# Recurrent gates on 64 x 64 quarters of TensorE, a weight tile for two blocks, and ScalarE's first copies and casts in program order

## The chip, the cores and the metric

The kernel runs on one core of one Trainium2 chip. Its engines are TensorE (PE, with its weight load PEld), VectorE (DVE), ScalarE (ACT), GpSimd (POOL) and SyncE (SP, which issues the DMAs here). The metric is the device time of one execution, in microseconds (us).

## The reference

Two layers of a hybrid model over 256 tokens and 256 context tokens, width 1024. Each layer normalises and modulates its input, projects it with one wide matrix, feeds three mixers (a bidirectional gated linear recurrence, retention, windowed attention), merges them and adds a mixture of 32 experts. The change lies in the norm's start and in the recurrence (LRU), whose gates are products with 16 matrices of 64 x 64, one for each head:

```python
def lru_scan(u, wa, ba, wx, bx, lam, h0, reverse):
    ub = u.reshape(B, L, LRU_HEADS, LRU_BW)                # 16 heads of 64
    r = jax.nn.sigmoid(jnp.einsum('blhi,hij->blhj', ub, wa).reshape(B, L, D_RNN) + ba)
    i = jax.nn.sigmoid(jnp.einsum('blhi,hij->blhj', ub, wx).reshape(B, L, D_RNN) + bx)
    log_a = -LRU_C * r * jax.nn.softplus(-lam)
    a = jnp.exp(log_a)
    b = jnp.sqrt(-jnp.expm1(2.0 * log_a)) * (i * u)
    a_cum, b_cum = lax.associative_scan(_linear_combine, (a, b), reverse=reverse, axis=1)
    return a_cum * h0[:, None, :] + b_cum
```

## The kernel before

Everything is kept transposed: channels on the 128 partitions, 512 tokens (context, then latent) along the free axis. Weights come in as fp32 tiles `raw` of 1 MB, and each half of one is split by ScalarE (`whi`, a cast) and VectorE (`wlo`, the rest), so that TensorE multiplies three times, `whi` with `uhi` and `ulo`, and `wlo` with `uhi`. `Dense.T` (L207 to L209) does that for 256 output channels in four groups of 12 matmuls, `Dense.N` (L258 to L260) for products with tokens on the partitions, and `Dense.first` (L238 to L240) for the first 512 channels of a layer, in two halves of the contraction, so that the second half of the norm's output may come later. In layer 0 `norm1` makes its scale and shift in two halves: `mod_half` multiplies four 1 MB tiles `wmod` by the condition (psmod, L441, four column tiles of the array), adds a bias on VectorE (modrow, L445), transposes on TensorE (pst, L447) and copies (modT, L450); ScalarE and VectorE then each modulate half the tokens (u, L561 and L562), and a cast and a subtraction make `uhi` and `ulo` (L488, L489). The second half runs as `between()` inside `first`.

`lru` runs four blocks of 256 channels. A block projects, convolves (`lu`, L606 on ScalarE and L610 on VectorE) and appends to a list `pend` four `gates(kk, di)`, one `root` and two `scan(kk)`; `tick()`, called after each group of 12 matmuls, takes one of them from the list. A gate is two fp32 matmuls of 128 x 128 by 512 (zr L622, zi L623; each shows as two records), two Tanh on the PSUM banks (tr L625, ti L631), a Tanh and an Exp (lT L627, lQ L628), and two VectorE steps. `root` is one Sqrt over a whole block (L648, behind a table load). `scan` is VectorE's row of products and scans (L655 to L667). Two heads share a 128 x 128 weight, whose other two quarters are zeros: `load_lru_w` has GpSimd clear the tile `lruw` (L578), and eight DMAs of 32 KB fill its diagonal, once for each block. Between these, single `psmod` groups (L412, from `mod_vec`) fill in as work that later stages need; each multiplies a 1 MB `wmod` tile, of which there are two buffers.

A scheduler sets one fixed order of instructions for each engine ahead of time, from the program, buffer sizes and its own costs; `tc.keep_in_program_order` holds chosen instructions in the order in which the program names them. Each DMA waits in SyncE's order. So what stands ahead of an instruction on its engine can hold it up.

## Time and profile before

| | |
|---|---|
| median of 3 runs | 2469.4 us (2464.6 to 2470.68) |
| the profiled execution | 2469.8 us, of which the span is 2468.0 |
| TensorE busy | 2332.3 us, 95% of the span |
| VectorE busy | 1273.3 us, 52% |
| ScalarE busy | 784.8 us, 32% |
| GpSimd busy | 69.9 us, 3% |

Busy times are averages over stages with different limits. The layer-0 recurrence lies at about 59 to 200 us of the span, that of layer 1 at about 1440 to 1612 us; the experts follow each. The rest of the kernel is not touched by the change.

### The profile page before, as it was taken

Reading aid. Unit: us, or ns where it says so; the run is one execution under the profiler, and the core shown is the slowest. Engines: PE = TensorE matmul, PEld = TensorE weight load, DVE = VectorE, ACT = ScalarE, POOL = GpSimd, SP = SyncE. Lnnn points to the kernel's source line nnn. Section 1 sums busy time; section 2 is a strip of 40 time slices with the busy share of each in tenths; the row PEclk is TensorE's granted clock in tenths of the full one; section 3 lists DMA queues with packets and bytes.
Section 4 is the critical chain, followed back from the end, with each engine's and each line's share of the span. In section 5 each row is a group of like instructions: output and inputs, shape, how many; then the busy total and the mean of one; then the engine's idle time right before and its main releaser. Section 6 shows DMA issues by size and latency. Waiting matters only on the chain. (4 is left out here: it accounts for less than half of the span.)

```text
span 2468.0 us, 33524 instructions
## 1 busy us (share of the span) xinstructions
PE 2332.3 (95%) x13576; PEld 1586.1 (64%) x13576; DVE 1273.3 (52%) x2458; ACT 784.8 (32%) x1397; POOL 69.9 (3%) x99
## 2 busy tenths in 40 slices
PE   6999999999999989998999989999999889989997
PEld 5667787888888964445444367788889844333433
DVE  4796444367764552324233678776787632222224
ACT  3665222255543321000000166744555411010001
POOL 1000000000000000000000110000000000000001
PEclk8999999999999979999999989999999989999999
DMA  8655353221323557999899932233334889999997
GB/s 291 234 188 198 132 187 102 86 86 52 96 86 106 186 219 303 398 389 376 364 399 415 376 99 90 86 103 120 120 104 147 311 344 405 419 383 420 420 420 293
DMA packets 203709, 589.44 MB, mean 239 GB/s; under 512 B 24112, under 2 KB 135328, under 8 KB 154656
## 3 DMA queue, kind: packets, MB, share of 16 engines
q1 hardware_dynamic: 203552, 587.26, 62.6%
q8 instruction: 109, 1.79, 0.3%
q14 instruction: 48, 0.39, 0.1%
HBM read 585.05 MB, written 2.16 MB: 238 GB/s over the span
## 5 line engine op out<-in xcount | busy, mean ns | idle before, releaser
L180 DVE TENSOR_TENSOR wlo<-raw,whi 128x1024 fp32r<-128x1024 f32 x212 | 258.9, 1222 | 215.6 <-ACT whi L179 209.6
L179 ACT CAST whi<-raw 128x1024 fp32r<-128x1024 f32 x212 | 222.5, 1050 | 353.6 <-PE pT L208 283.3
L207 PE MATMUL pT<-uhi,whi 128*128 128x512 f32 (+1 forms) x896 | 331.0, 370 | 2.3 <-ACT uhi L488 2.3
L209 PE MATMUL pT<-uhi,wlo 128*128 128x512 f32 (+1 forms) x896 | 315.6, 352 | 0.0
L208 PE MATMUL pT<-ulo,whi 128*128 128x512 f32 (+1 forms) x896 | 315.0, 352 | 0.0
L1239 PE MATMUL pdn<-we,hT 128*64 128x512 f32 x1024 | 260.6, 607 | 35.9 <-DMA we<-in_expert_w_down_dram 35.9
L1239 PE MATMUL pup<-we,xT 128*64 128x512 f32 x1024 | 231.5, 593 | 1.5 <-DMA we<-in_expert_w_up_dram 1.5
L1239 PE MATMUL pgate<-we,xT 128*64 128x512 f32 x1024 | 231.0, 603 | 0.0
L1239 PEld LDWEIGHTS pdn<-we,hT 128*64 128x64 f32 x1024 | 83.7, 139 | 203.4 <-issue 129.5
L207 PEld LDWEIGHTS pT<-uhi,whi 128*128 128x128 f32 x896 | 169.7, 190 | 39.0 <-issue 12.6
L208 PEld LDWEIGHTS pT<-ulo,whi 128*128 128x128 f32 x896 | 169.8, 190 | 26.1 <-issue 4.9
L209 PEld LDWEIGHTS pT<-uhi,wlo 128*128 128x128 f32 x896 | 169.3, 189 | 25.1 <-issue 1.1
L1328 ACT CAST myh<-pdn 128x512 fp32r<-128x512 f32 x64 | 37.6, 587 | 457.2 <-PE pdn L1239 457.2
L1239 PEld LDWEIGHTS pup<-we,xT 128*64 128x64 f32 x1024 | 75.2, 137 | 150.7 <-issue 143.7
L1239 PEld LDWEIGHTS pgate<-we,xT 128*64 128x64 f32 x1024 | 71.3, 139 | 140.1 <-issue 137.2
L258 PE MATMUL pN<-whi,uhi 128*128 128x256 f32 x512 | 151.2, 295 | 0.0
L259 PE MATMUL pN<-wlo,uhi 128*128 128x256 f32 x512 | 145.6, 284 | 5.6 <-DVE wlo L180 5.5
L1329 DVE TENSOR_TENSOR myl<-pdn,myh 128x512 fp32r<-128x512 f32 x64 | 44.0, 688 | 198.1 <-ACT myh L1328 198.1
L260 PE MATMUL pN<-whi,ulo 128*128 128x256 f32 x512 | 145.4, 284 | 0.0
L207 PE MATMUL pT<-yhi,whi 128*128 128x512 f32 (+1 forms) x384 | 132.4, 345 | 0.0
L209 PE MATMUL pT<-yhi,wlo 128*128 128x512 f32 (+1 forms) x384 | 129.4, 337 | 0.0
L208 PE MATMUL pT<-ylo,whi 128*128 128x512 f32 (+1 forms) x384 | 129.4, 337 | 0.0
(335 smaller groups left out, 3995.6 us busy)
## 6 DMA issues: line engine op xcount, KB each, us to landing
we<-in_expert_w_down_dram SPq DMA_DIRECT2D x128, 1024.0 KB
we<-in_expert_w_gate_dram SPq DMA_DIRECT2D x127, 1024.0 KB
we<-in_expert_w_up_dram SPq DMA_DIRECT2D x125, 1024.0 KB
raw<-in_w_in_dram SPq DMA_DIRECT2D x76, 1024.0 KB
wmod<-in_w_mod_dram SPq DMA_DIRECT2D x48, 1024.0 KB
raw<-in_w_branch_a_dram SPq DMA_DIRECT2D x8, 1024.0 KB
raw<-in_w_branch_b_dram SPq DMA_DIRECT2D x8, 1024.0 KB
raw<-in_w_branch_c_dram SPq DMA_DIRECT2D x8, 1024.0 KB
```

The costliest lines, as they stand in the source:

```text
L179: act.copy(hi, raw[:, 4 * kh:4 * kh + 4])
L180: dve.tensor_sub(lo, raw[:, 4 * kh:4 * kh + 4], hi.bitcast(F32))
L207: pe.matmul(ps[j], wh, xhi(kk)[:, n0:n1], start=kk == 0, stop=False)
L208: pe.matmul(ps[j], wh, xlo(kk)[:, n0:n1], start=False, stop=False)
L209: pe.matmul(ps[j], wl, xhi(kk)[:, n0:n1], start=False, stop=kk == 7)
L258: pe.matmul(ps[:, i], xh, wh, start=kk == 0, stop=False)
L259: pe.matmul(ps[:, i], xh, wl, start=False, stop=False)
L260: pe.matmul(ps[:, i], xl, wh, start=False, stop=kk == 7)
L1239: keep(pe.matmul(*a, **k))
L1328: act.copy(yh[:, cc], pd)
L1329: dve.tensor_sub(yl[:, cc], pd, yh[:, cc].bitcast(F32))
```

## The change

Four edits go together. (1) `lruw` holds the matrices of two blocks without zeros, [128, 4, 4, 64]; eight DMAs of 64 KB fill it, for blocks 0 and 1 ahead of the norm and for blocks 2 and 3 in block 1; the clearing on GpSimd is gone. (2) A gate is four matmuls of 64 x 64 by 512 on the four quarters of the array: zr on (0, 0) and (64, 64), zi on (0, 64) and (64, 0), so that zi's two halves come out with their partitions exchanged. (3) ti's Tanh is two instructions on 64 partitions each, reading the exchanged halves. (4) `Dense.half` makes the parts of `first`; its casts are held in program order, as are the first copies of `norm1` (L546), and the first half of the first weight tile is cast ahead of the first modulation.

```diff
+        def half(self, c, kh):
+            raw = self.raws[c][:, 4 * kh:4 * kh + 4]
+            hi = T("ws", [P, 4, 256], F32R, name="whi")
+            lo = T("ws", [P, 4, 256], F32R, name="wlo")
+            tc.keep_in_program_order(act.copy(hi, raw))
+            dve.tensor_sub(lo, raw, hi.bitcast(F32))
+            return hi, lo
...
-                    act.copy(hi, self.raws[c][:, 4 * kh:4 * kh + 4])
-                    dve.tensor_sub(lo, self.raws[c][:, 4 * kh:4 * kh + 4], hi.bitcast(F32))
-                    parts.append((hi, lo))
+                    parts.append(self.early.pop() if kh + c == 0 else self.half(c, kh))
...
-                (act.copy if k % 2 else dve.tensor_copy)(us[k], pss[k])
+                tc.keep_in_program_order((act.copy if k % 2 else dve.tensor_copy)(us[k], pss[k]))
         if early:
             vectors(0)
+            dns[0].early = [dns[0].half(0, 0)]
...
-        wb = lru_w[L, c] = T("t4", [P, 2, 4, P], name="lruw")
-        ms = pool.memset(wb, 0.0)
-        if L and c == 0:
-            tc.keep_in_program_order(ms)
+        wb = T("t4", [P, 4, 4, 64], name="lruw")
+        for i in range(2):
+            lru_w[L, c + i] = wb[:, 2 * i:2 * i + 2]
...
-        if c < 3:
-            load_lru_w(L, c + 1)
+        if c == 1:
+            load_lru_w(L, 2)
...
-            pe.matmul(zr, wb[:, kk, 2 * di], uf, start=True, stop=True)
-            pe.matmul(zi, wb[:, kk, 2 * di + 1], uf, start=True, stop=True)
+            for h, z in ((0, zr), (1, zr), (0, zi), (1, zi)):
+                r, o = 64 * h, 64 * (h if z is zr else 1 - h)
+                pe.matmul(z[o:o + 64], wb[r:r + 64, kk, 2 * di + (z is zi)], uf[r:r + 64], start=True, stop=True,
+                          tile_position=(r, o))
...
-            act.activation(ti, zi, AF.Tanh, scale=0.5, bias=vt[:, 64 + 8 * di + k:65 + 8 * di + k])
+            for r in (0, 64):
+                act.activation(ti[r:r + 64], zi[64 - r:128 - r], AF.Tanh, scale=0.5,
+                               bias=vt[r:r + 64, 64 + 8 * di + k:65 + 8 * di + k])
```

The order of instructions moves at three places. In the listings a row gives the line, the operation, and its output and inputs by name with a running number.

The first is VectorE at the first modulation of layer 0, before:

```order
L362 COPY lam_92<-vec_245 128x16
L445 TENSOR_TENSOR modrow_316<-psmod_251,bmod_96 128x128
L450 COPY modT_55_320<-pst_318 128x4x2
L557 SCALAR_TENSOR_TENSOR a_50_249<-modT_55_320,vec_245 128x2x4
L445 TENSOR_TENSOR modrow_322<-psmod_250,bmod_110 128x128
L450 COPY modT_58_326<-pst_324 128x4x2
L562 TENSOR_SCALAR u_231<-u_231,a_50_249,modT_58_326 128x256 x2
```

and after:

```order
L367 COPY lam_92<-vec_244 128x16
L219 TENSOR_TENSOR wlo_249<-raw_124,whi_248 128x1024
L450 TENSOR_TENSOR modrow_319<-psmod_254,bmod_96 128x128
L450 TENSOR_TENSOR modrow_325<-psmod_253,bmod_110 128x128
L455 COPY modT_57_323<-pst_321 128x4x2
L563 SCALAR_TENSOR_TENSOR a_52_252<-modT_57_323,vec_244 128x2x4
L455 COPY modT_60_329<-pst_327 128x4x2
```

The first `wlo`, which needs the first `raw` tile and its cast, now stands ahead of both modrow; before, it came well behind the four modulations.

The second place is the second half of `first` in layer 0. TensorE before:

```order
L441 MATMUL psmod_466<-wmod_134,sT 32x128 x16
L447 MATMUL pst_534<-cst,modrow_532 128x128
L447 MATMUL pst_539<-cst,modrow_537 128x128
L238 MATMUL pT_406<-uhi_189,whi_559 128x512
L238 MATMUL pT_407<-uhi_189,whi_559 128x512
L238 MATMUL pT_408<-uhi_189,whi_563 128x512
```

TensorE after:

```order
L452 MATMUL pst_523<-cst,modrow_521 128x128
L452 MATMUL pst_528<-cst,modrow_526 128x128
L417 MATMUL psmod_572<-wmod_573,sT 32x256 x8
L243 MATMUL pT_399<-uhi_188,whi_548 128x512
L244 MATMUL pT_399<-ulo_189,whi_548 128x512
L243 MATMUL pT_400<-uhi_188,whi_548 128x512
L244 MATMUL pT_400<-ulo_189,whi_548 128x512
L417 MATMUL psmod_572<-wmod_595,sT 32x256
```

SyncE's issues that feed it, before:

```order
L170 DMA raw_567<-in_w_in_dram 128x8x256
L170 DMA raw_569<-in_w_in_dram 128x8x256
L310 DMA wmod_584<-in_w_mod_dram 128x2x1024
L310 DMA wmod_606<-in_w_mod_dram 128x2x1024
L323 DMA bmod_638<-in_b_mod_dram 4x256 x2
L310 DMA wmod_628<-in_w_mod_dram 128x2x1024
```

and after:

```order
L128 DMA am_390<-in_const_dram 128x256
L1050 DMA br_7739<-in_router_group_b_dram 128x4
L1050 DMA br_7739<-in_router_expert_b_dram 128x32
L315 DMA wmod_573<-in_w_mod_dram 128x2x1024
L315 DMA wmod_595<-in_w_mod_dram 128x2x1024
L315 DMA wmod_617<-in_w_mod_dram 128x2x1024
L170 DMA raw_556<-in_w_in_dram 128x8x256
L170 DMA raw_558<-in_w_in_dram 128x8x256
```

Two psmod groups with new wmod tiles now stand ahead of or among the first matmuls of that half; SyncE issues those tiles ahead of the two `raw`, behind `am` and two small loads (`br`). Before, both groups came behind the half. On ScalarE the last two casts of `first` (whi_548 and whi_552 after, whi_559 and whi_563 before), which stood ahead of the second modulation, now stand behind it.

The third place is ScalarE at the end of the last LRU block of layer 0, its last two gates and what follows, before:

```order
L625 ACTIVATE tr_1618<-zr_1614,vec_245 128x512
L631 ACTIVATE ti_1623<-zi_1615,vec_245 128x512
L627 ACTIVATE lT_1551<-tr_1618,spm 128x512
L628 ACTIVATE lQ_1552<-tr_1618,spm 128x512
L625 ACTIVATE tr_1644<-zr_1640,vec_245 128x512
L631 ACTIVATE ti_1649<-zi_1641,vec_245 128x512
L627 ACTIVATE lT_1551<-tr_1644,spm 128x512
L628 ACTIVATE lQ_1552<-tr_1644,spm 128x512
L494 ACTIVATE rk_1652<-pT_1537 128x512
```

and after:

```order
L631 ACTIVATE tr_1640<-zr_1634,vec_244 128x512
L638 ACTIVATE ti_1645<-zi_1635,vec_244 64x512
L633 ACTIVATE lT_1565<-tr_1640,spm 128x512
L634 ACTIVATE lQ_1566<-tr_1640,spm 128x512
L638 ACTIVATE ti_1645<-zi_1635,vec_244 64x512
L631 ACTIVATE tr_1669<-zr_1663,vec_244 128x512
L638 ACTIVATE ti_1674<-zi_1664,vec_244 64x512
L633 ACTIVATE lT_1565<-tr_1669,spm 128x512
L634 ACTIVATE lQ_1566<-tr_1669,spm 128x512
L638 ACTIVATE ti_1674<-zi_1664,vec_244 64x512
L499 ACTIVATE rk_1678<-pT_1551 128x512
```

Each gate has one ti more, and `rk`, the first ScalarE step of the retention, now follows all eight halves of the block. In blocks 1 and 2 the gates have the same form, and a cast `whi` with its `wlo`, which stood among the gates, now stands between `lu` and the table load.

## Rows read from the trace of the kernel before

**Rows 1.** Windows, layer 0: stretch, us, then each engine's busy us

```profile
98.00:133.00 35.00, 35.00 (x182) 23.27 (x181) 31.14 (x47) 23.43 (x31) 0.31 (x1) 1.00 0.56 190
```

**Rows 2.** Timeline (start us, duration us, instruction), ScalarE, one layer-0 LRU block

```profile
115.59 0.81 ACT L627 ACTIVATE lT<-tr,spm 128x512 f32<-128x512 f32 x1
...
117.01 0.67 ACT L631 ACTIVATE ti<-zi,vec 128x512 f32<-128x512 f32 x1
117.58 0.67 ACT L625 ACTIVATE tr<-zr,vec 128x512 f32<-128x512 f32 x1
...
150.81 0.81 ACT L627 ACTIVATE lT<-tr,spm 128x512 f32<-128x512 f32 x1
```

**Rows 3.** Timeline, VectorE, the same block's scan

```profile
130.99 0.68 DVE L655 SCALAR_TENSOR_TENSOR lT<-lQ,lT 128x512 f32<-128x512 f32 x1
```

**Rows 4.** Timeline, TensorE, first gates of blocks 1 and 2 of layer 0

```profile
106.40 1.02 PE L622 MATMUL zr<-lu,lruw 128*128 128x512 f32 x2
...
140.37 1.02 PE L622 MATMUL zr<-lu,lruw 128*128 128x512 f32 x2
```

**Rows 5.** Timeline, TensorE, the first work behind the layer-0 LRU

```profile
196.34 1.18 PE L498 MATMUL prot<-rk,dcr 128*128 128x256 f32 x4 [2.11 <-ACT rk L494]
```

**Rows 6.** Groups by line and form, ScalarE: 64 partitions, then 128

```profile
L929 ACT CAST aq<-aq 64x512 fp32r<-64x512 f32 x16 | 9.9, 620 | 15.1 <-DVE aq L502 14.9
...
L952 ACT CAST yhi<-ya 128x512 fp32r<-128x512 f32 x8 | 4.5, 617 | 0.0
```

**Rows 7.** Timeline, TensorE, the first gate of layer 0 and what surrounds it

```profile
66.10 1.07 PE L412 MATMUL psmod<-wmod,sT 128*32 128x256 f32 x16
67.10 0.50 PE L207 MATMUL pT<-uhi,whi 128*128 128x512 f32 x1
67.44 0.39 PE L208 MATMUL pT<-ulo,whi 128*128 128x512 f32 x1
67.67 0.40 PE L209 MATMUL pT<-uhi,wlo 128*128 128x512 f32 x1
...
71.19 1.02 PE L622 MATMUL zr<-lu,lruw 128*128 128x512 f32 x2
72.05 1.02 PE L623 MATMUL zi<-lu,lruw 128*128 128x512 f32 x2
73.00 1.07 PE L412 MATMUL psmod<-wmod,sT 128*32 128x256 f32 x16
```

**Rows 8.** Timeline, TensorE, first gates of two successive blocks of layer 1

```profile
1497.03 1.10 PE L622 MATMUL zr<-lu,lruw 128*128 128x512 f32 x2 [0.86 <-issue]
...
1535.49 1.10 PE L622 MATMUL zr<-lu,lruw 128*128 128x512 f32 x2 [0.74 <-ACT rv L778]
```

**Rows 9.** Timeline, ScalarE, one of the waits inside that block

```profile
1504.56 0.69 ACT L625 ACTIVATE tr<-zr,vec 128x512 f32<-128x512 f32 x1 [0.28 <-PE zr L622]
```

**Rows 10.** Timeline, TensorE, between the start and the second half of `first`

```profile
23.76 1.94 PE L441 MATMUL psmod<-wmod,sT 128*32 128x128 f32 x32 [3.06 <-DMA wmod<-in_w_mod_dram]
...
32.10 0.79 PE L238 MATMUL pT<-uhi,whi 128*128 128x512 f32 x1 [5.11 <-ACT whi L225]
...
34.19 0.79 PE L240 MATMUL pT<-uhi,wlo 128*128 128x512 f32 x1 [0.87 <-DVE wlo L226]
...
54.74 1.20 PE L238 MATMUL pT<-uhi,whi 128*128 128x512 f32 x4 [1.90 <-ACT uhi L488]
```

**Rows 11.** Timeline, ScalarE, the same stretch

```profile
26.95 1.09 ACT L561 ACTIVATE u<-u,modT,a 128x256 f32<-128x256 f32 x2 [8.14 <-DVE modT L450]
...
35.79 1.99 ACT L225 CAST whi<-raw 128x1024 fp32r<-128x1024 f32 x2 [1.17 <-DMA raw<-in_w_in_dram]
```

**Rows 12.** Timeline, SyncE's issues, the weights behind the first half

```profile
51.80 1.73 SPq L170 DMA_DIRECT2D raw<-in_w_in_dram  x2
```

**Rows 13.** DMA in 40 slices of 0.5 us, from 50 to 70 us

```profile
GB/s 81 15 6 64 36 60 150 207 315 381 389 369 334 272 276 350 362 354 377 389 401 410 401 410 410 410 434 401 358 191 74 0 0 0 0 0 106 106 303 377
```

**Rows 14.** Windows: busy time of each engine, granted clock (PEclk), at layer 1's start

```profile
1434.00:1440.00 6.00, 5.99 (x15) 4.77 (x16) 5.99 (x12) 4.85 (x10) 0.00 (x0) 0.51 0.23 50
```

More of the change, by code (lines that the diff above doesn't have):

```diff
@@ L222, in first @@
                 for c in range(2):
-                    hi = T("ws", [P, 4, 256], F32R, name="whi")
-                    lo = T("ws", [P, 4, 256], F32R, name="wlo")
-                    act.copy(hi, self.raws[c][:, 4 * kh:4 * kh + 4])
-                    dve.tensor_sub(lo, self.raws[c][:, 4 * kh:4 * kh + 4], hi.bitcast(F32))
-                    parts.append((hi, lo))
+                    parts.append(self.early.pop() if kh + c == 0 else self.half(c, kh))
                 if kh:
@@ L583, in load_lru_w @@
                 for par in range(2):
-                    nc.sync.dma_start(
-                        wb[64 * par:64 * par + 64, :, 2 * di + ty, 64 * par:64 * par + 64],
-                        A[nm][L, di, 4 * c + par:4 * c + 4:2].rearrange("k i j -> i k j"))
+                    nc.sync.dma_start(wb[64 * par:64 * par + 64, :, 2 * di + ty],
+                                      A[nm][L, di, 4 * c + par:4 * c + 8:2].rearrange("k i j -> i k j"))
     def lru(L, dn, u, q0, between):
```

## The prediction

> **What bounds the kernel now.** I read the windows first, then the timelines of the stretches that the change touches, engine by engine, then the groups by form for prices. In the layer-0 recurrence TensorE shows no gap: 35.00 us busy of 35.00, with ScalarE at 23.43 [rows 1]. That looks like a stretch in which shorter matmuls are worth their whole length. The timelines say otherwise. From lT of one block to lT of the next, ScalarE and VectorE form a closed chain: ScalarE runs four gates without a gap from 115.59 on, then lu, a table load and the Sqrt [rows 2]; VectorE's scan takes over at 130.99 [rows 3] and runs without a gap to gx, ScalarE's gx and a cast follow, and the next lT starts at 150.81 [rows 2]. That is 35.22 us a block, more than TensorE's own period, 33.97 from the first gate of block 1 to that of block 2 [rows 4]. At the end TensorE indeed waits 2.11 us for ScalarE's rk [rows 5]. In layer 1 the chain closes through TensorE: first gates of two blocks are 38.46 us apart [rows 8], and TensorE waits inside. So in blocks 1 to 3 of both layers ScalarE's time counts, and TensorE's does so only in the first block, where ScalarE waits for each zr, and where gates hold ScalarE up.
>
> **Part 1, the gates on TensorE.** zr and zi start 0.86 us apart, so a gate takes 1.72, of two passes of 0.43 for each matrix [rows 7]. No row of before shows quarters. The nearest are column tiles: psmod, 16 records of 256 columns on four column tiles, takes 1.00 us from its start to the next matmul [rows 7]; at 0.215 a pass, four at a time make 0.86, so four column tiles run at once, with 0.14 for changing the array's form; 0.09 more ahead of the group (zi to psmod takes 0.95 instead of 0.86) and 0.11 behind it (67.10 to 67.44 is 0.34, the next step to 67.67 only 0.23) make 0.35. If four quarters run at once, a gate is 0.86 + 0.35 = 1.21, a gain of 0.51, or 16.3 us over 32 gates. If two do, 2.07, a loss of 0.35; if none do, 3.44 + 0.35, a loss of 2.07. The trace has no two row tiles next to each other, so it can't show how they do together. I take 1.21, since psmod is nearest in kind, and keep the others as a rival. Little of the gain lies on the path: three gates of block 0 in each layer, 3 x 0.51 = 1.5 us, and in layer 1 the waits of ScalarE for zr and zi within a block, of which one shows 0.28 [rows 9] and the three together 0.6.
>
> **Part 2, ti in halves.** On ScalarE a cast of 64 x 512 takes 620 ns, one of 128 x 512 takes 617 [rows 6]: partitions are free, and a half costs what the whole did. The step from ti to the next instruction is 0.57 us [rows 2]. Bounds: nothing, if halves went twice as fast, which those rows exclude, and 0.67, the duration. Four gates a block add 4 x 0.57 = 2.3 us, back to back, ahead of the Sqrt. In block 0 only the last half counts, 0.57. The cover that could hide this, ScalarE's idle time during the scan, lies behind the chain's next step, since lT stands behind gx in the order.
>
> **Part 3, casts moved in blocks 1 and 2.** whi now stands between lu and the table load; that leaves ScalarE's sum as it was, but its wlo comes on VectorE ahead of the scan's first step, and by my chain ends some 0.3 later than the Sqrt. Another wlo goes into the scan's stretch (about 1.15) while its whi leaves the place ahead of lT (about 0.95): +0.2. Together +0.5 for each of the two.
>
> **Part 4, the start of layer 0.** Before, modrow ended the wait and u began at 26.95 [rows 11]. Now the first wlo stands ahead of both modrow on VectorE, and its wait for raw holds them, pst on TensorE, u on ScalarE and all behind. When does raw land? Its predecessor landed at 23.76 [rows 10], the raw three tiles later at 35.79 [rows 11]: 12.03 us for 4 MB, about 3.0 each, so 26.8. The cast and wlo need about 2.6 more, so modrow comes at 29.4 and u at about 30.9, nearly 4 us later. Against this the cast is done, and TensorE's first half, which began at 32.10 [rows 10] and then stopped for wlo to 34.19 [rows 10], begins at about 32.5 and has no such stop: it ends some 1.5 us earlier, near 47, and the second u comes near 51.6. But the casts whi that stood ahead of that modulation are now behind it, so TensorE has both operands near 56.8, against 54.74 [rows 10]. Worse, two psmod groups stand there with wmod tiles that SyncE has only just issued. Before, it issued two raw at 51.80 [rows 12] and two wmod behind them, and those 4 MB moved from about 53 to 65 us [rows 13]: summing the slices, the first MB is in at about 56 and each further one takes some 2.6. Now wmod goes first, behind two small loads, at about 52.6, lands near 57, and the second near 59.7; the second group stands behind only four matmuls. So TensorE goes on at about 60, where before it was a microsecond past 54.74: some 4.5 later, with zr at about 76 (71.19 before [rows 7]). Since one psmod group more (1.1 us) is by then done, I count +3.7. Bounds: 0, if wmod lands at once, and +7, if the clock falls in the idle stretch before; at the start of layer 1, behind a stretch with long waits, 6 us ran at a granted 0.51, half speed [rows 14], which would cost 3 us.
>
> **Part 5, the weights.** GpSimd's clearing and half the DMA issues go. No row shows a matmul that waits for lruw, and the same 2 MB without zeros move. I cost it at nothing; the cover is that lruw is loaded tens of us ahead.
>
> **The sum**, against the profiled execution of 2469.8 us (0.4 above the median of the runs):
> - start: +3.7
> - layer 0, block 0: -1.5 + 0.57 = -0.9
> - layer 0, blocks 1 to 3: 3 x 2.3 + 2 x 0.5 = +7.9. It is seen at prot, behind rk, which now waits for eight halves; TensorE's 8 us of shorter gates become wait.
> - layer 1: -0.9 in block 0, and 3 x (2.3 - 0.6) = +5.1 in the others: +4.2
>
> Together +14.9, or 2484.7. Behind the recurrences TensorE is busy without a gap again, so nothing gives this back.
>
> **The rivals.** *The quarters do not run at once.* For it: the trace shows only column tiles at once [rows 7]. With pairs, block 0 costs 3 x 0.35 + 0.57 = 1.6 in each layer, layer 0's blocks hide the rest under the chain, and in layer 1 ScalarE waits as before and 0.35 longer for the first gate: 3.7 + 1.6 + 7.9 + 1.6 + 3 x 2.65 = +22.8, or 2492. If zr's two quarters and zi's two exclude each other, their order leaves three slots, 2.58 + 0.35 = 2.93 a gate, 1.21 more than now. TensorE's layer-0 blocks are then 38.8 us, which beats the chain: 3.7 + 16 x 1.21 + 0.6 - 2.1 = 21.6 there, and some 14.7 in layer 1 (3 x 1.21 + 0.57 in block 0, 3 x (2.3 + 1.2) behind it), which gives 2506. The Trainium skill speaks for this: "TensorEngine Tiling (Array Packing)", section Restrictions and Gotchas, says that different row tiles cannot access the same PSUM bank simultaneously, and here both banks take one quarter from each half of the rows. No row of before can show whether that holds.
>
> *TensorE sets the pace* (the other side). ScalarE is busy 23.43 of 35 us [rows 1], so 2.3 more would fit. If the scan is not what lT waits for, all 16.3 us count, less 3.7 at the start: 2457. It decides at one point, whether lT comes before the previous block's gx on ScalarE; the order says it doesn't, and 2.11 us of wait [rows 5] speak against it too.
>
> *The start gains instead.* If raw lands by 24, VectorE's wlo is done before modrow is due, u stays at 26.95, and the stop between 32.10 and 34.19 is gone; the start gives 3 to 5 us and the recurrences take it back with 11: within 0.3%, 2472 to 2477.
>
> **How the numbers follow.** 0.3% is 7.4 us, about what a measurement of this kernel can tell from no change. The forecast, 2478 to 2491, has a chance of 0.58; quarters one behind another, 2492 to 2506, 0.15; the start that gains, or halves that fall into gaps I don't see, 0.15; TensorE's pace, 2457, 0.12. So faster 0.12, same 0.15, slower 0.73. I predict 2484.7. The range, 2466 to 2499, leaves out TensorE's pace and the slowest quarters.
>
> **What would show it.** Right: prot waits over 8 us for rk; lT to lT is about 38 us in layer 0; zi's quarters overlap zr's, and a gate takes about 1.2; the first u starts near 31 and the second half's matmuls stop for a wmod. Wrong: no wait at prot, TensorE without gaps through both recurrences, or a gate of 2 us and more. The weakest steps are the landing times of raw and wmod, which I inferred from the rate, and the quarters.

## The result, and the profile after

The changed kernel takes 2491.8 us (median of 4, 2488.5 to 2493.5) against 2468.3 for the kernel before (median of 4): a ratio of 1.0095, with an interval of 1.0079 to 1.0111. It is slower, as forecast (2484.7), and 7 us more so. The profiled execution has a span of 2488.4 (2468.0 before), so 20.4 us can be followed through the traces (prs is the first product of the retention; the last of these is the last one on the line of the first, L707 before and L715 after):

| stage, us of the span | before | after | difference |
|---|---|---|---|
| first zr of layer 0 starts at | 71.2 | 76.9 | +5.7 |
| from there to the first prs, the layer-0 recurrence | 175.5 | 184.7 | +9.2 |
| from there to the first zr of layer 1 | 1209.8 | 1202.8 | -7.0 |
| from there to the last prs, the layer-1 recurrence and the retention behind it | 242.7 | 255.3 | +12.5 |
| the rest | 768.8 | 768.8 | 0.0 |

The first group of the page gives busy time, share and instructions of each engine:

```profile
PE 2324.1 (93%) x13704; PEld 1571.5 (63%) x13704; DVE 1272.9 (51%) x2458; ACT 809.6 (33%) x1429; POOL 61.6 (2%) x91
```

TensorE has 8.2 us less to do than before and ScalarE 24.8 more, yet the time follows ScalarE. The first gate on quarters, TensorE's timeline (start us, duration us, instruction; a count behind x takes records together):

```profile
76.85 0.65 PE L628 MATMUL zr<-lu,lruw 64*64 64x512 f32 x2
76.87 0.65 PE L628 MATMUL zi<-lu,lruw 64*64 64x512 f32 x2
77.33 0.59 PE L628 MATMUL zr<-lu,lruw 64*64 64x512 f32 x2
77.35 0.60 PE L628 MATMUL zi<-lu,lruw 64*64 64x512 f32 x2
77.87 0.42 PE L417 MATMUL psmod<-wmod,sT 128*32 128x256 f32 x4
```

All four quarters start within 0.02 us, in two passes, and the next matmul starts 1.02 us after the first, where zr and zi took 1.81 to the next psmod before [rows 7]. ScalarE's timeline, from one lT of block 1 of layer 0 on, with a whole gate from 124.10 to 127.64, and the lT of the next block:

```profile
119.85 0.81 ACT L633 ACTIVATE lT<-tr,spm 128x512 f32<-128x512 f32 x1
...
124.10 0.80 ACT L633 ACTIVATE lT<-tr,spm 128x512 f32<-128x512 f32 x1
124.80 0.81 ACT L634 ACTIVATE lQ<-tr,spm 128x512 f32<-128x512 f32 x1
125.63 0.68 ACT L638 ACTIVATE ti<-zi,vec 64x512 f32<-64x512 f32 x1
126.34 0.69 ACT L631 ACTIVATE tr<-zr,vec 128x512 f32<-128x512 f32 x1
127.06 0.69 ACT L638 ACTIVATE ti<-zi,vec 64x512 f32<-64x512 f32 x1
127.64 0.80 ACT L633 ACTIVATE lT<-tr,spm 128x512 f32<-128x512 f32 x1
...
159.01 0.80 ACT L633 ACTIVATE lT<-tr,spm 128x512 f32<-128x512 f32 x1
```

The gate takes 3.54 us, and lT to lT 39.16, against 35.22 before [rows 2]. What ScalarE takes longer, TensorE waits for: its zr now stops for a ti that has not yet freed its PSUM bank, once in each of blocks 1 to 3 (TensorE's timeline, the wait and its releaser in brackets). The windows (length of the stretch, then busy us of PE, PEld, DVE, ACT and POOL with their counts, granted clock, DMA share, GB/s) show the idle time of the third block and the clock that goes down with it, on average to 0.91 of full speed:

```profile
122.82 1.08 PE L628 MATMUL zr<-lu,lruw 64*64 64x512 f32 x4 [1.16 <-ACT ti L638]
...
161.97 1.12 PE L628 MATMUL zr<-lu,lruw 64*64 64x512 f32 x2 [4.37 <-ACT ti L638]
...
201.12 1.12 PE L628 MATMUL zr<-lu,lruw 64*64 64x512 f32 x2 [3.71 <-ACT ti L638]
```

```profile
159.01:198.16 39.15, 35.44 (x192) 21.20 (x192) 31.28 (x48) 26.99 (x36) 0.31 (x1) 0.91 0.57 189
```

The -7.0 between the recurrences, where the change edits only layer 1's start (its first casts and the clearing), goes with the granted clock. TensorE runs the same matmuls there and is idle 1.0 us less, but busy 6.0 us less. The windows of that stretch, before and after, in the columns given above:

```profile
246.67:1456.47 1209.80, 1168.45 (x6505) 795.47 (x6505) 580.00 (x1126) 311.37 (x608) 39.42 (x47) 0.98 0.59 226
```

```profile
261.53:1464.31 1202.78, 1162.48 (x6506) 789.08 (x6505) 579.36 (x1126) 310.78 (x608) 35.32 (x43) 0.98 0.60 227
```

Summed from the traces, the clock was at half speed for 58.0 us of it before and for 41.0 after (0.976 and 0.983 on average; the windows round both to 0.98). The kernels of the experiments show the same relation (e1, whose experts differ, left out):

| half speed between the recurrences, us | 37.5 | 41.0 | 44.4 | 51.2 | 58.0 |
|---|---|---|---|---|---|
| kernels | e2, e9 | after, e5, e7, e11 | e4, e8 | e6, e10, e12 | before, e3 |
| length of the stretch, us | 1201.3, 1204.6 | 1202.8, 1201.9, 1202.0, 1203.3 | 1203.5, 1205.4 | 1207.2, 1213.4, 1210.8 | 1209.8, 1210.9 |

Why the clock fell for a longer or a shorter time was not tested.

The start: ScalarE's first u, VectorE's wait for the mask `am`, SyncE's issue of the first wmod, and TensorE's stop for it:

```profile
29.89 0.60 ACT L567 ACTIVATE u<-u,modT,a 128x256 f32<-128x256 f32 x1 [2.52 <-DVE modT L455]
...
51.11 0.29 DVE L129 CAST amr<-am 128x256 fp32r<-128x256 f32 x1 [9.38 <-DMA am<-in_const_dram]
...
50.39 8.76 SPq L315 DMA_DIRECT2D wmod<-in_w_mod_dram  x3
...
56.80 1.94 PE L417 MATMUL psmod<-wmod,sT 128*32 128x256 f32 x16 [4.61 <-DMA wmod<-in_w_mod_dram]
```

### The profile page after: what moved, and what is told of

It is laid out like the page before. It is cut to its first block, busy times and chain, and to the rows that moved or that the text cites. A ratio compares the mean times of both kernels' runs of the same rounds, so it can differ in the third digit from the quotient of the medians.

```text
span 2488.4 us, 33740 instructions
## 1 busy us (share of the span) xinstructions
PE 2324.1 (93%) x13704; PEld 1571.5 (63%) x13704; DVE 1272.9 (51%) x2458; ACT 809.6 (33%) x1429; POOL 61.6 (2%) x91
## 5 line engine op out<-in xcount | busy, mean ns | idle before, releaser
L1336 ACT CAST myh<-pdn 128x512 fp32r<-128x512 f32 x64 | 37.5, 586 | 457.1 <-PE pdn L1247 457.1
```

The lines of the kernel that those rows point to most:

```text
L1336: act.copy(yh[:, cc], pd)
```

## The experiments

The questions were: what of the loss are ti's halves, and is it the halves or the exchange (e1, e2, e3); what holds the start (e4 to e7, e9, e10); can the exchange be had elsewhere (e8); where do the 7 us between the recurrences come from (e11); and do start and halves add (e12).

### e1, ti whole, the exchange left out

```diff
-            for r in (0, 64):
-                act.activation(ti[r:r + 64], zi[64 - r:128 - r], AF.Tanh, scale=0.5,
-                               bias=vt[r:r + 64, 64 + 8 * di + k:65 + 8 * di + k])
+            act.activation(ti, zi, AF.Tanh, scale=0.5, bias=vt[:, 64 + 8 * di + k:65 + 8 * di + k])
```

> The changed kernel with one edit: ti is one Tanh over 128 partitions again, while the gates stay on four quarters. So ti gets zi's halves without their exchange; that part of the computation is left out. Theory A, the halves of ti are what made the recurrences longer (in the trace of the changed kernel a gate takes 3.54 us on ScalarE instead of 2.56, 0.98 more, 3.9 a block): lT to lT in layer 0 falls from 39.2 to about 35.2, rk comes 12 us earlier, three blocks of layer 1 give 3.9 each, and the two first blocks 0.8 each; about 24 us in all, so 2468 us. Theory B, halves cost 0.57 a gate as predicted, 2.3 a block, and the rest comes from the new order of casts: 15 us, 2477. Theory C, the quarters themselves hold things up: no gain, 2491.

2516.0 us (ratio 1.0198). The total means nothing here: without the exchange the gates, and with them the tokens' experts, differ, and the expert part of layer 0 is the longer one. The stages ahead of it do compare. The layer-0 recurrence takes 172.8, against 184.7 in the changed kernel and 175.5 before; layer 1's takes 239.5, against 255.3 and 242.7. ScalarE's two lT, its timeline:

```profile
120.17 0.81 ACT L633 ACTIVATE lT<-tr,spm 128x512 f32<-128x512 f32 x1
...
155.32 0.81 ACT L633 ACTIVATE lT<-tr,spm 128x512 f32<-128x512 f32 x1
```

35.15 apart, 4.01 less than in the changed kernel. Block by block the halves cost 1.6, 4.0, 4.0 and 2.2 us in layer 0 and 2.5, 5.0, 4.2 and 4.0 in layer 1, together 11.8 and 15.7. The rest of the change gains 2.6 and 3.2 against the kernel before; 1.1 of the 2.6 is a psmod group that is done ahead of the first zr. Two things changed along with the halves: the cast whi stands among the gates again, as before (so e1 doesn't by itself refute theory B's order of casts; the part on the prediction does that from other rows), and layer 1's recurrence has 10 us at half clock where the changed kernel has 24, so that its 15.7 holds some of the clock.

### e2, both gates on the diagonal quarters, ti whole

```diff
-                r, o = 64 * h, 64 * (h if z is zr else 1 - h)
-                pe.matmul(z[o:o + 64], wb[r:r + 64, kk, 2 * di + (z is zi)], uf[r:r + 64], start=True, stop=True,
-                          tile_position=(r, o))
+                r = 64 * h
+                pe.matmul(z[r:r + 64], wb[r:r + 64, kk, 2 * di + (z is zi)], uf[r:r + 64], start=True, stop=True,
+                          tile_position=(r, r))
...
-            for r in (0, 64):
-                act.activation(ti[r:r + 64], zi[64 - r:128 - r], AF.Tanh, scale=0.5,
-                               bias=vt[r:r + 64, 64 + 8 * di + k:65 + 8 * di + k])
+            act.activation(ti, zi, AF.Tanh, scale=0.5, bias=vt[:, 64 + 8 * di + k:65 + 8 * di + k])
```

> The changed kernel with the gates on two diagonal quarters only, (0, 0) and (64, 64), for zr and zi alike, and ti whole; the output is complete. A gate should take about 1.8 us on TensorE instead of 1.02, since only two quarters run at once. Theory A (ScalarE's chain sets the pace, TensorE's gate time counts only in the first blocks and at each first gate of layer 1): 2 x 3 x 0.75 = 4.5 us and 3 x 0.75 = 2.3 us above e1_whole, so about 2475. Theory C' (TensorE's gates set the pace, four quarters are worth their 0.75 x 32): 24 us above e1_whole, so 2492.

2474.7 us (median of 10), ratio 1.0032, 1.0022 to 1.0043: 17 us less than the changed kernel, and what the theory of the halves gave. TensorE's first gate, then ScalarE's lT of two gates and of the next block:

```profile
80.38 1.08 PE L628 MATMUL zr<-lu,lruw 64*64 64x512 f32 x4
81.29 1.02 PE L628 MATMUL zi<-lu,lruw 64*64 64x512 f32 x4
82.25 1.07 PE L417 MATMUL psmod<-wmod,sT 128*32 128x256 f32 x16
```

```profile
124.67 0.81 ACT L633 ACTIVATE lT<-tr,spm 128x512 f32<-128x512 f32 x1
...
127.80 0.81 ACT L633 ACTIVATE lT<-tr,spm 128x512 f32<-128x512 f32 x1
...
130.35 0.81 ACT L633 ACTIVATE lT<-tr,spm 128x512 f32<-128x512 f32 x1
...
159.87 0.81 ACT L633 ACTIVATE lT<-tr,spm 128x512 f32<-128x512 f32 x1
```

With only two quarters at a time a gate is longer than before on TensorE (in layer 1 zr to zr 4.86, before 4.51), and still the block of layer 0 falls to 35.20: TensorE's gate doesn't set it. In layer 1 it does count: the recurrence takes 245.9 there, 6.3 more than in e1. A gate on ScalarE is 2.55, as before. The casts that the change moved stand here as in the kernel before, whi among the gates, so e2 doesn't test them.

### e3, the kernel before with ti in two halves, not exchanged

```diff
-            act.activation(ti, zi, AF.Tanh, scale=0.5, bias=vt[:, 64 + 8 * di + k:65 + 8 * di + k])
+            for r in (0, 64):
+                act.activation(ti[r:r + 64], zi[r:r + 64], AF.Tanh, scale=0.5,
+                               bias=vt[r:r + 64, 64 + 8 * di + k:65 + 8 * di + k])
```

> The kernel before with one edit: ti is two Tanh on 64 partitions each, not exchanged. Theory A: 3.9 us in each of six blocks and about 0.8 in each first block, 25 us, so 2493; in the timeline ScalarE's step from tr to a half of ti is 0.71 us, as in the changed kernel, where it was 0.57. Theory B: 0.57 a gate and no more, 2.3 x 6 + 1.1 = 15 us, 2483. Theory D, the exchange (reading partitions 64 to 127 and writing 0 to 63) is what costs the additional 0.14 us a step: steps of 0.57 here, and 2483.

2486.1 us, ratio 1.0075 (1.0059 to 1.0092), between the figures; the total doesn't decide, since the order of the blocks changed too (lT to lT is 37.53, then 39.12; whi stands behind lu, as in the changed kernel). ScalarE's steps do:

```profile
118.75 0.80 ACT L627 ACTIVATE lT<-tr,spm 128x512 f32<-128x512 f32 x1
119.45 0.80 ACT L628 ACTIVATE lQ<-tr,spm 128x512 f32<-128x512 f32 x1
120.28 0.68 ACT L632 ACTIVATE ti<-zi,vec 64x512 f32<-64x512 f32 x1
120.99 0.69 ACT L625 ACTIVATE tr<-zr,vec 128x512 f32<-128x512 f32 x1
121.58 0.67 ACT L632 ACTIVATE ti<-zi,vec 64x512 f32<-64x512 f32 x1
122.15 0.81 ACT L627 ACTIVATE lT<-tr,spm 128x512 f32<-128x512 f32 x1
```

A gate takes 3.40. The half on partitions 64 to 127 (the one behind lQ) costs 0.83 to enter and 0.71 to leave; the half on 0 to 63 (behind tr) 0.59 and 0.57, as a whole ti would. So of the 0.98 us that a gate gained in the changed kernel, 0.57 is the instruction, 0.27 the half that starts at partition 64, and 0.14 the exchange: there the half that reads from 64 and writes to 0 also costs 0.72 (126.34 to 127.06) to enter. Halves as such are 86% of it. These are no single steps: in the changed kernel each of the 32 from lQ to a half takes 0.82 or 0.83, where the 16 from lQ to a whole ti take 0.70 or 0.71 in the kernel before.

### e4, the mask's load behind the layer-0 recurrence

```diff
-        else:
-            load_mask()
         load_tables()
         early, late = retention(L, dn, u, q0)
         ya = lru(L, dn, u, q0, early)
+        if L == 0:
+            load_mask()
```

> The changed kernel with one edit: the mask am is loaded and cast behind the recurrence of layer 0 instead of ahead of it. In the changed kernel VectorE waits 9.38 us for am ahead of the second modrow, which comes at 51.32 instead of about 49. Theory E (the second half of the first product waits for its wmod tile, landed at 56.8, whatever the modulation does): u starts near 50, but the second half still starts between 56 and 57, and the time is 2491, within 1 us. Theory F (the chain modrow, u, uhi, whi sets the start): zr and the end come 2.3 us earlier, 2489.

2494.3 us, ratio 1.0110 (1.0093 to 1.0127), 3 more than theory E had. VectorE's wait of 9.38 for `am` is gone and the second modulation's u starts at 49.88 instead of 52.51, but TensorE then waits the longer for wmod:

```profile
59.32 1.93 PE L417 MATMUL psmod<-wmod,sT 128*32 128x256 f32 x16 [9.68 <-DMA wmod<-in_w_mod_dram]
```

The mask's stall was covered. That the first zr is even later (79.51) follows the issue of that wmod, at 52.84 here and at 50.39 in the changed kernel.

### e5, without the early cast

```diff
-                    parts.append(self.early.pop() if kh + c == 0 else self.half(c, kh))
+                    parts.append(self.half(c, kh))
...
-            dns[0].early = [dns[0].half(0, 0)]
```

> The changed kernel without its early cast: the first half of the first weight tile is cast inside `first` again, held in program order, so that no wlo stands ahead of the two modrow on VectorE. Theory W (the start is set by the two psmod fills, whose wmod tiles are issued ahead of the second pair of raw): u goes back to about 27, TensorE's first half begins near 32 with a stop for wlo of about 2 us, but the second half still waits for wmod, goes on at 58 to 60, and the first zr stays at 76 to 78; total 2491, within 2 us of the changed kernel. Theory E (the wait for raw ahead of modrow is what the start costs): the first zr comes at 73 to 74, total about 2488.

2496.2 us (2 runs), ratio 1.0117 (1.0079 to 1.0154), outside the 2 us that theory W gave itself. The mechanism is that of theory W: the first half begins at 33.10, behind a whi, and the second half waits for wmod all the same, with the first zr at 80.28, later than W's 76 to 78. Across the kernels whose second half begins with that psmod, the first zr follows the issue of its wmod to within 1.0 us, whatever else was edited:

| | after | e1 | e11 | e4 | e5 | e2 |
|---|---|---|---|---|---|---|
| first of the wmod issued at | 50.39 | 51.88 | 51.69 | 52.84 | 53.09 | 54.18 |
| first zr | 76.85 | 78.79 | 78.78 | 79.51 | 80.28 | 80.38 |
| difference | 26.5 | 26.9 | 27.1 | 26.7 | 27.2 | 26.2 |

The order of SyncE's queue is nearly the same in all; the profile of the changed kernel happens to hold the earliest issue of the six.

### e6, the fills held behind each group of matmuls

```diff
-                            pe.matmul(ps[c][j], wl, xhi(kk), start=False, stop=kk == 7)
+                            m = pe.matmul(ps[c][j], wl, xhi(kk), start=False, stop=kk == 7)
+                            if self.hold and kk == 7:
+                                tc.keep_in_program_order(m)
...
-                    pe.matmul(ps[32 * g:32 * g + 32], sT[:, 2 * kq + k], w[:, k, g * SEG:(g + 1) * SEG],
+                    m = pe.matmul(ps[32 * g:32 * g + 32], sT[:, 2 * kq + k], w[:, k, g * SEG:(g + 1) * SEG],
                               start=(kq == 0 and k == 0), stop=(kq == 3 and k == 1), tile_position=(0, 32 * g))
+                    if L == 0 and i == 2:
+                        tc.keep_in_program_order(m)
```

> The changed kernel with the psmod fills of the second half held behind the last matmul of each group of 12, so that TensorE's second half no longer begins behind a psmod. Theory W (the fills' wmod is the wait): the wait of 4.61 us for wmod is gone, the second half begins when whi is cast behind the last uhi, near 57.6, the first zr at 74 to 75.5, total 2489 to 2490. Rival C (the held casts and the mask's wait would have ended no sooner, and the fills only filled an idle stretch): the second half begins at 57.6 at half clock and waits for wmod after 12 matmuls instead, first zr 76 to 77, total 2491 to 2493.

2500.6 us (2 runs), ratio 1.0134: slower than either expected. TensorE's waits:

```profile
58.58 0.80 PE L243 MATMUL pT<-uhi,whi 128*128 128x512 f32 x1 [5.46 <-ACT whi L218]
...
72.64 1.07 PE L419 MATMUL psmod<-wmod,sT 128*32 128x256 f32 x16 [0.45 <-DMA wmod<-in_w_mod_dram]
...
78.72 0.65 PE L633 MATMUL zr<-lu,lruw 64*64 64x512 f32 x2
```

As rival C had it, the cast held behind the second modulation was as late as wmod, so that the fill had only stood in a stretch that was idle anyway. But that makes 1.9 us at the first zr; some 9 more stand in the span behind it, where nothing was edited: 4.4 between the recurrences and 5.4 behind the layer-1 one. They go with the granted clock, which was at half speed for 51 us in each of these two stretches, against 41 and 38 in the changed kernel.

### e7, e2 with another start

To e6's holds on e2 come: the second half's casts ahead of its modulation, u's modulation and the casts of the weight tile behind `first` in program order, and the mask later.

```diff
-                if kh:
-                    self.between()
                 for c in range(2):
                     parts.append(self.early.pop() if kh + c == 0 else self.half(c, kh))
                 if kh:
+                    self.between()
+                if kh:
...
+                if early:
+                    tc.keep_in_program_order(ua)
```

> The kernel of e2 (both gates of a head pair on the diagonal quarters, ti whole) with another start: the casts of the second half of `first` ahead of its modulation, the psmod fills held behind matmuls, u's modulation held in order, the mask's load behind the layer-0 recurrence. If the start loses by these orders, as I hold: the second half begins near 52.5 without a wait for wmod, the first zr at 69 to 71 instead of 80.4, and the total is 2474.7 - 9.5 = 2465 (2462 to 2468), 1 to 2 us under the kernel before. If the start's loss lies in the DMA order alone (raw and wmod land when they land): first zr 77 to 80, total 2472 to 2475.

2474.8 us (median of 12), ratio 1.0033: no gain over e2. TensorE's timeline:

```profile
50.92 1.19 PE L245 MATMUL pT<-uhi,whi 128*128 128x512 f32 x4 [1.55 <-ACT uhi L499]
...
61.95 1.94 PE L421 MATMUL psmod<-wmod,sT 128*32 128x256 f32 x16 [6.09 <-DMA wmod<-in_w_mod_dram]
...
76.95 0.65 PE L637 MATMUL zr<-lu,lruw 64*64 64x512 f32 x2
```

The second half now begins 3.8 us earlier than in the kernel before [rows 10], and stops in its middle instead: with raw ahead of wmod in SyncE's queue, wmod lands later still. The first zr missed its 69 to 71.

### e8, the exchange made by GpSimd at the input

```diff
+            ux = T("t2", [P, 512], name="lux")
+            for r in (0, 64):
+                pool.tensor_copy(ux[r:r + 64], us[kk][64 - r:128 - r])
+            uxs.append(ux)
...
+                r, o = 64 * h, 64 * (h if z is zr else 1 - h)
+                pe.matmul(z[o:o + 64], wb[r:r + 64, kk, 2 * di + (z is zi)], (uf if z is zr else uxs[kk])[r:r + 64],
+                          start=True, stop=True, tile_position=(r, o))
```

> The kernel of e7 with the gates on four quarters, and the exchange taken out at the input instead of at the output: GpSimd copies each lu with its two halves of the partitions exchanged, zi multiplies that copy by weights loaded on exchanged partitions, and zi comes out in place, so ti is one instruction. Theory A (the halves on ScalarE are what the quarters cost): the layer-0 recurrence from the first zr to the first prs as in e1, 172.8 (e2 175.1), layer 1's 239.6 (e2 245.9); 8.6 less than e7, or 2456 (2453 to 2460). Rival P (GpSimd's copies hold VectorE up, as its clearing of lruw held xn, 0.75 to 3.19 us): VectorE's rows beside the copies grow to 2 us and more, and as VectorE is in the chain of each block the 32 copies cost 0.5 us each: total 2472 or more.

2482.2 us, ratio 1.0055 (1.0036 to 1.0073): 7.4 more than e7, on the rival's side. ScalarE's gate is 2.55 again, but lT to lT is 37.42, then 38.36, where e7 had 35.20 and 36.41. One of VectorE's groups from 121 to 195 us, of e7 and then of e8:

```profile
L670 DVE SCALAR_TENSOR_TENSOR lT<-lQ,lT 128x512 f32<-128x512 f32 x8 | 5.5, 683 | 0.0
```

```profile
L675 DVE SCALAR_TENSOR_TENSOR lT<-lQ,lT 128x512 f32<-128x512 f32 x8 | 7.0, 893 | 1.7 <-ACT lT L668 1.7
```

Only some rows that fall beside a copy are longer (in this group four, which take 1.09 to 1.14 instead of 0.68), less than the rival's 2 us a row. They make 0.8 of the 2.0 to 2.2 us by which a block is longer than in e7. The order also changed: three of VectorE's lu now stand among the scan's first steps. The copies cost more than they saved; how much of the rest is order stays open.

### e9, e7 without fills in the second half

```diff
-                        if kh:
+                        if kh and not self.hold:
                             tick()
```

> The kernel of e7 without any psmod fill inside the second half of `first`; the three groups that stood there come later. In e7 the second half began at 50.92 (54.74 in the kernel before) and then waited 6.09 us for wmod inside. Theory W (the fills' wmod is what holds the first zr in every version so far): no wait for wmod ahead of the first zr, which comes at 66 to 69 instead of 76.95. Three groups of 1.07 us have then still to be done, so that of the 9 us about 6 stay: total 2469 (2466 to 2471). Rival R (the raw tiles behind the second half are next: their casts stand behind the second modulation's): first zr 72 to 76, total 2472 to 2475.

2460.6 us (median of 11), ratio 0.9977 (0.9966 to 0.9989): faster than both kernels, and 14 us less than e2, more than I expected. TensorE goes from the start of the second half to the first gate without a stop:

```profile
50.92 1.19 PE L245 MATMUL pT<-uhi,whi 128*128 128x512 f32 x4 [1.55 <-ACT uhi L499]
...
65.08 1.07 PE L637 MATMUL zr<-lu,lruw 64*64 64x512 f32 x4
```

The first zr is 15.3 us earlier than in e2, and the recurrence takes 174.9, no longer than there. But the three groups of psmod did not find room: the recurrence holds 21 groups in both kernels, and the last three of e9's run between the recurrences, which takes 3.3 us longer than in e2 at the same 37.5 us of half clock, or 1.1 a group. Behind the layer-1 recurrence e9 is 2.5 shorter than e2, with 45.5 us at half clock instead of 52.5.

### e10, the kernel before with e9's start

Its gates are the whole matrices of before, with GpSimd's clearing and a tile for each block; the start is that of e9, with the edits of e6 and e7 and this:

```diff
             vectors(0)
+            dns[0].early = [dns[0].half(0, 0)]
+            dns[0].hold = True
...
-                        if kh:
+                        if kh and not self.hold:
                             tick()
```

> The kernel before, its gates and its lruw as they were, with the start of e9: early cast and early casts of the second half, held copies, no fill inside the second half, the mask's load behind the layer-0 recurrence. Theory W: first zr at 66 to 69 (71.19 before) and one psmod group less done by then (1.07), so 1 to 4 us faster than the kernel before: 2463 to 2466. Rival R: first zr 71 to 74, total 2467 to 2471.

2473.5 us, ratio 1.0019 (1.0005 to 1.0034). The first zr came at 67.30, as W had it, and the time didn't follow:

```profile
67.30 1.02 PE L637 MATMUL zr<-lu,lruw 128*128 128x512 f32 x2
...
74.55 1.44 PE L421 MATMUL psmod<-wmod,sT 128*32 128x256 f32 x16 [2.57 <-DMA wmod<-in_w_mod_dram]
...
80.00 1.02 PE L637 MATMUL zr<-lu,lruw 128*128 128x512 f32 x2
```

Here SyncE issues the wmod only at 66.79, behind the lruw of the next block and a raw that goes at 66.30 (in e9 that wmod went at 53.27, with 16 lruw ahead of it and not 24, and without that raw), and the second gate waits for it. The span is 4.5 us longer than before, in four parts: the first zr is 3.9 earlier, the layer-0 recurrence takes 1.7 more, the stretch between the recurrences 3.6 more, with three psmod groups more in it (3.2), and the end 3.1 more, with 52 us at half clock instead of 38.

### e11, e2 with layer 1's clearing put back

```diff
         wb = T("t4", [P, 4, 4, 64], name="lruw")
+        for n in range(4 * (L and c == 0)):
+            tc.keep_in_program_order(pool.memset(wb, 0.0))
```

> The kernel of e2 with GpSimd's clearing of lruw put back at layer 1's start only (four clearings of 128 x 1024, held in program order, as in the kernel before). If the clearing holds VectorE: the last xn of layer 1 takes 3 us and more instead of 0.75, psu waits 1.4 to 2.4 us more, and from the first psu to the first pT of layer 1 it takes 10.1 to 11 us instead of 7.7. If the long xn has another cause: 0.75 and 7.7 as in e2.

2472.5 us (one run). The question came from layer 1's norm, where in the kernel before one VectorE row is four times as long as its like while GpSimd clears lruw; in the changed kernel it isn't. VectorE's last xn before, after, and in e11, each from its own timeline:

```profile
1427.39 3.19 DVE L530 TENSOR_SCALAR xn<-h,rs 128x1024 f32<-128x1024 f32 x1 [0.72 <-POOL rs L149]
```

```profile
1438.66 0.75 DVE L535 TENSOR_SCALAR xn<-h,rs 128x1024 f32<-128x1024 f32 x1 [0.72 <-POOL rs L149]
```

```profile
1430.77 1.41 DVE L535 TENSOR_SCALAR xn<-h,rs 128x1024 f32<-128x1024 f32 x1 [0.71 <-POOL rs L149]
```

The row gets longer again, but to 1.41 and not to 3, and from the first psu to the first pT it takes 8.36, against 7.71 in e2 and 10.14 before. Half confirmed: the clearing does hold VectorE, and how long varies (e3 and e10, which keep the clearing, show 4.08). The lengths are steps of 0.89, the time from one of the four clearings to the next: xn ends 0.55 behind the end of the first of them in e11, of the third before, and of the fourth in e3 and e10.

### e12, the changed kernel with e9's start

The edits of e6 and e7 on the changed kernel, and e9's:

```diff
-                        if kh:
+                        if kh and not self.hold:
                             tick()
```

> The changed kernel, its gates on four quarters and ti in exchanged halves, with the start of e9. If start and halves add (Theory S): the first zr at 65 to 67 instead of 76.85, and the total falls by what e9 gained over e2 (14.1), to 2477.7 (2475 to 2481); the rest of the way to e9's 2460.6, 17 us, is the halves. lT to lT in layer 0 stays 39.2. If the idle time of TensorE in the recurrence swallows an earlier start (Theory G): the total stays above 2484.

2480.2 us, ratio 1.0047 (1.0027 to 1.0066): inside theory S's range, 11.5 less than the changed kernel, with the first zr at 65.2. lT to lT is 39.48. To e9 it is 19.6 more, and not all of that is the halves: between the two profiles 6.8 us lie in the layer-0 recurrence and 8.3 in layer 1's, but 6.2 in the stretch between the two, where e12 has 51 us at half clock and e9 38. Against the changed kernel the first zr is 11.7 earlier and the layer-0 recurrence 3.0 shorter, and the stretch behind it 8.0 longer, with three psmod groups more and 51 us at half clock instead of 41.

## Why the prediction was right, and where its steps were off

**What bounds the kernel** was right, and it made the sign. The closed chain through ScalarE and VectorE sets the blocks of layer 0; e2 lengthens TensorE's gate and leaves the block at 35.2, e1 shortens it and leaves it there too. That the forecast came within 7 us is in part luck, since two misses cancel:

| term, us | forecast | shown |
|---|---|---|
| start, with one psmod group (1.1) done early | +3.7 | +4.6 |
| layer-0 recurrence | +7.0 | +10.3 (halves +11.8, gates -1.5) |
| layer-1 recurrence | +4.2 | +12.5 (halves +15.7, the rest -3.2) |
| between the recurrences | 0 | -7.0 |
| sum | +14.9 | +20.4 |

The group that moved ahead of the first zr is counted with the recurrence in both columns.

**Part 1.** Four at once, as taken. Beside a psmod, which has tiles too, the gate is 1.02; between two groups of pT in layer 1 it takes 4.01 from zr to zr where it took 4.51, a gain of 0.50 where 0.51 was forecast. What it brings on the path, 1.5 us in layer 0 (e1's 2.6 less the psmod group's 1.1) and 3.2 in layer 1 is what the sum had, 1.5 and 3.3, though these figures hold all that the change does to the recurrences except the halves. The rival by the Trainium skill ("TensorEngine Tiling (Array Packing)", Restrictions and Gotchas, that different row tiles cannot access the same PSUM bank simultaneously) doesn't show: zr's two quarters, on different rows and in one bank, start together (76.85).

**Part 2 is the term that was mis-sized.** I took 0.57 for a half from the step of whole instructions [rows 2]; it is 0.98, so 3.9 a block instead of 2.3. The price of 64 partitions that I read [rows 6] was that of an instruction's duration, in a row of its like, not that of the step between instructions that start at partition 0 and at 64. And in block 0 I counted one half only, 0.57, where by e1 it pays 1.6 in layer 0 and 2.5 in layer 1. Together the halves cost 11.8 and 15.7, where the sum had 7.5 for each layer. Layer 1's excess alone is more than the 7 us by which the forecast fell short.

**Part 3** was too high by about 1 us. The Sqrt and the scan's first step in block 1, before (ScalarE) and after (ScalarE, then VectorE):

```profile
128.98 1.91 ACT L648 ACTIVATE lT<-lT 128x2048 f32<-128x2048 f32 x1
```

```profile
137.12 1.92 ACT L656 ACTIVATE lT<-lT 128x2048 f32<-128x2048 f32 x1
...
139.34 0.68 DVE L663 SCALAR_TENSOR_TENSOR lT<-lQ,lT 128x512 f32<-128x512 f32 x1
```

From the block's first lT the Sqrt comes after 17.27 instead of 13.39, the scan after 19.49 instead of 15.40 [rows 2] [rows 3], the next block after 39.16 instead of 35.22. So 3.88 of the 3.94 are there ahead of the Sqrt, where four gates with 0.98 more make 3.92. The wlo that now stands ahead of the scan holds it by 0.2, where 0.3 was forecast, and the rest of the block gives that back. So the moved casts cost less than 0.1 us in this block, and theory B of e1 is out.

**Part 4** held almost row by row: first u at 29.89 (30.9 forecast), wmod at 56.80 (57), first zr at 76.85 (76). What I missed is `am`, which SyncE issues behind 16 lruw instead of 8, and which holds the second modrow to 51.32; e4 shows that wmod covers it. The +3.7 credited a psmod group that was done early. That was right: the layer-0 recurrence holds 21 groups instead of 22, e1's gain there is 1.1 more than the 1.5 of three gates, and e9's three groups cost 3.3 us where they went. So +5.7 at the first zr is +4.6 of loss. By the table under e5 the first zr scatters by 3.5 us with the issue of one wmod, and the changed kernel's profile is the earliest; that may be why the medians lie 23.5 apart and the two spans 20.4.

**Part 5** was wrong in sign, within what is shown: 2.4 of the 7.0 us that came back between the recurrences is the last xn without clearing (10.14 to 7.71 from psu to pT). Another 2.4 lies ahead of the experts, with 13.7 us at half clock instead of 23.9, 1.2 in them, with 19.4 instead of 21.6, and 1.0 behind that pT, with 3.4 instead of 5.8. e12 has no clearing and takes 1210.8 there, as before, with three psmod groups more and 51 us at half clock, so the 7 us are not a sure gain of the change. The sentence that nothing would give time back behind the recurrences did not hold for this execution.

**The sign that I named** was wrong: prot waits 1.13 us, not 8. The 9.2 us of wait stand at zr, behind ti, because halves that end late free their bank late. TensorE's spare time is where it next needs something of the slow engine, not at the end of the stage.

## What to carry to other kernels

When two engines form a closed loop through a stage, an edit that moves work from the third engine onto one of the two can lose, as here, however much the third is busy; read the loop's period before the busy shares. Price an added instruction by the step to its neighbours, in the same mix of partitions, and not by its own duration. And a filler that needs a load of its own belongs behind the critical stretch, not in it: taking three of them out of the second half of `first` was worth more (14 us from e7 to e9) than any order of casts, and gave the fastest kernel of the study. It is no rule: in e10 the first zr came 3.9 us earlier and the time did not fall, since the next wmod was issued 13.5 us later than in e9. And a few us that appear where nothing was edited are to be held against the granted clock before another cause is looked for.

## What the hardware showed

An activation on 64 partitions that reads or writes from partition 64 on starts 0.13 to 0.15 us later behind one on 128 partitions, and the next starts 0.14 later behind one that wrote there (the changed kernel and e3); on partitions 0 to 63 neither shows (e3). I had not expected the start partition to matter.

GpSimd's clearing held a VectorE operation on SBUF for 0.7 to 3.3 us (0.75 alone; 1.41, 3.19 and 4.08 beside it), by one, three and four clearings that follow each other every 0.89 us: VectorE did not always get its turn behind the first. The Trainium skill ("SBUF — State Buffer", section "SBUF: two separate sides") says that the two share a port pair that one of them takes for a whole instruction; the rows agree, and show that the one that waits can miss its turn between two clearings.
